# One layer of a streaming-encoder trunk on one core: gate and up weights, from the second strip on, split into a ring of four buffers, each strip at its own byte position

## The chip, the cores and the metric

The kernel runs on one core of a Trainium2 chip. The metric is the device time of one execution in microseconds (us). The core has five engines that run beside each other and wait for each other by semaphores: TensorE (PE; matrix products, with PEld for the loading of the stationary operand), VectorE (DVE), ScalarE (ACT), GpSimd (POOL) and SyncE (SP), which here issues the transfers from HBM. Matrix operands lie in SBUF (128 partitions, each a row of bytes), results in PSUM banks of 512 float32 per partition.

## The reference

All data are float32, 512 tokens of width 1024. What is computed is

```python
h = x + mixer(rms_norm(x))              # forgetting attention, latent attention, gates, output projection
hn = rms_norm(h, norm_ffn_g)
h = h + (silu(hn @ w_ffn_gate) * (hn @ w_ffn_up)) @ w_ffn_down     # hidden width 2816
y = rms_norm(h, norm_final_g)
```

The change concerns the two products `hn @ w_ffn_gate` and `hn @ w_ffn_up` (1024 by 2816 each).

## The kernel before

Float32 accuracy is made from three products in the type float32r. `split` (L98) writes a rounded copy `hi` of an operand (ScalarE, L101) and the remainder `lo = source - hi` (VectorE, L102). `mm3` (L124) adds hi·hi, hi·lo and lo·hi into one PSUM bank: three matmuls, the first operand stationary, the second streamed through the array. So each matmul is preceded by a load of 128 stationary columns, which is 512 bytes per partition, and streams up to 512 columns.

The feed-forward part starts after the mixer. `hTh` and `hTl` hold the normalised activations transposed, eight feature tiles of 128 features by 512 tokens, reached by `ht(k)`. The hidden width of 2816 is worked off in eleven strips of 256 (`NHC // 2`, loop at L935). For each strip the gate product goes into two PSUM banks (`pg`, tag a), the up product into two others (`pu`, tag b); then ScalarE takes silu of `pg`, VectorE multiplies by `pu`, and the result is split into `act[s]` (L947 to L951). The weights are the stationary operand: `strip` (L928) runs over the eight feature tiles k, over the two halves e of the strip and over the three products, 48 matmuls for one matrix of one strip. Strip 0 works in two halves of 256 tokens, because its activations arrive late; the other ten strips stream all 512 tokens, so that 20 times 48 matmuls of 512 columns follow each other.

`strip_weights` (L924) brings a matrix of a strip in two pieces of four feature tiles: `weights` (L130) takes a raw buffer (tag `wr`, two buffers), issues the transfer of 512 KB on SyncE's queue (L133), and `split_weights` (L136) takes a buffer `whi` and a buffer `wlo` (tags `wh` and `wl`, three of each) and splits. Strip 0 puts one piece into two buffers of tag `pt`. Tag `pt` has four buffers of `PTW` = 1664 float32 (6656 bytes), which the mixer used for attention weights and which hold the four normalised row tiles `hn` (L912) when the feed-forward part starts. After strip 0 they lie unused.

In the program's layout of SBUF the tiles that matter here (`wh`, `wl`, `pt`, the activations and `act`) all begin at byte 192 of a stretch of 512 bytes, and the blocks of 128 stationary columns inside them are whole multiples of 512 bytes further on. So every weight load of the feed-forward part starts at the same position in 512 bytes. The one large group of matmuls whose streamed operand starts elsewhere is the narrow input projection (`pms`, bank names `pm`, 424 columns): its weights lie 1696 bytes apart, so that feature tiles 0 to 3 start at bytes 192, 352, 0 and 160 of 512, and tiles 4 to 7 again.

The order on each engine is made by a planner that simulates the program; the mixer's matmuls are kept in written order (`pin`), the feed-forward part is left to the planner. Matmuls of one bank stay in order. The down product (L956 on) takes its weights by `weights` again, now as the streamed operand.

Of the kernel before, what the change touches and what calls it, by code (L numbers as in the profile page):

```python
# [8 lines left out]
F32 = mybir.dt.float32  # L9
F32R = mybir.dt.float32r  # L10
# [6 lines left out]
P = 128  # L17
D = 1024
S = 512
NT = S // P  # L20
KC = D // P
# [18 lines left out]
PTW = 3 * PTS + S  # L40
# [26 lines left out]
def tile_hybrid_fox_mla_block(  # L67
# [6 lines left out]
    nc = tc.nc  # L74
# [6 lines left out]
    w_ffn_gate, w_ffn_up, w_ffn_down = w_ffn_gate[0], w_ffn_up[0], w_ffn_down[0]  # L81

    big = ctx.enter_context(tc.tile_pool(name="big", bufs=1))
    ps = ctx.enter_context(tc.tile_pool(name="ps", bufs=1, space=bass.MemoryType.PSUM))

    def u8(shape, dtype, name):
        return big.tile(shape, dtype, name=name, tag="u8", bufs=17)
# [4 lines left out]
    def tmp(shape, name, dtype=F32):  # L92
        return big.tile(shape, dtype, name=name, tag="p", bufs=4)

    def bank(tag, name):
        return ps.tile([P, 512], F32, name=name, tag=tag, bufs=3 if tag == "a" else 5)

    def split(hi, lo, src, scale=None):  # L98

        if scale is None:  # L100
            one = nc.scalar.copy(out=hi, in_=src)  # L101
            two = nc.vector.tensor_tensor(out=lo, in0=src, in1=hi.bitcast(F32), op=ALU.subtract)  # L102
        else:
            one = nc.scalar.activation(out=hi, in_=src, func=AF.Copy, scale=scale)
            two = nc.vector.scalar_tensor_tensor(out=lo, in0=src, scalar=scale, in1=hi.bitcast(F32),
                                                 op0=ALU.mult, op1=ALU.subtract)
        if pin[1]:
            tc.keep_in_program_order(one)
            tc.keep_in_program_order(two)
# [4 lines left out]
    def matmul(*args, **kw):  # L114
        ins = nc.tensor.matmul(*args, **kw)  # L115
        if pin[0]:
            tc.keep_in_program_order(ins)
# [6 lines left out]
    def mm3(o, a, b, start, stop):  # L124

        matmul(o, lhsT=a[0], rhs=b[0], start=start, stop=False)
        matmul(o, lhsT=a[0], rhs=b[1], start=False, stop=False)
        matmul(o, lhsT=a[1], rhs=b[0], start=False, stop=stop)

    def weights(src, a, b, spare=False):  # L130

        raw = big.tile([P, a, b], F32, name="wraw", tag="wr", bufs=2)
        nc.sync.dma_start(out=raw, in_=src)  # L133
        return split_weights(raw, spare)
# [189 lines left out]
    for st in "f0 k0 f1 t0 k1 f2 t1 f3 t2 m1 t3 f4 t4 m2 t5 f5 f6 t6 f7 m3 t7 w0 w1".split():  # L324
        n = int(st[1])
# [10 lines left out]
        else:  # L336

            src = xf[n // 4][:, n % 4, :]
# [547 lines left out]
    def ht(k, cols=slice(None)):  # L886
        return hTh[k // 4][:, k % 4, cols], hTl[k // 4][:, k % 4, cols]
# [3 lines left out]
    for half in range(2):  # L891
        nn = slice(half * 512, (half + 1) * 512)
        wo = []
        for c in range(2):
            hi = u8([P, 4, 512], F32R, f"woh{half}{c}")
            lo = u8([P, 4, 512], F32R, f"wol{half}{c}")
            for d in range(2):
                raw = big.tile([P, 2, 512], F32, name="wraw", tag="wr", bufs=2)
# [4 lines left out]
        for t in range(NT):  # L903
            po = bank("a", "po")
            cols = slice(t * P, (t + 1) * P)
            for k in range(KC):
                c, kk = k // 4, k % 4
# [16 lines left out]
    def strip_weights(src, s, spare=False):  # L924
        return [weights(src[c * 512:(c + 1) * 512, s * 256:(s + 1) * 256].rearrange("(k p) n -> p k n", p=P), 4, 256,
                        spare and c == 1) for c in range(2)]

    def strip(po, w, cols):  # L928
        for k in range(KC):
            for e in range(2):  # L930
                c = slice(e * P, (e + 1) * P)
                mm3(po[e][:, cols], (w[k // 4][0][:, k % 4, c], w[k // 4][1][:, k % 4, c]), ht(k, cols),
                    k == 0, k == KC - 1)

    for s in range(NHC // 2):  # L935

        pg, pu = [bank("a", "pg") for _ in range(2)], [bank("b", "pu") for _ in range(2)]
        wg = strip_weights(w_ffn_gate, s)
        if s == 0:
            wu = strip_weights(w_ffn_up, s, spare=True)  # L940
            for cols in (slice(0, S // 2), slice(S // 2, S)):
                strip(pg, wg, cols)
                strip(pu, wu, cols)
        else:
            strip(pg, wg, slice(0, S))
            strip(pu, strip_weights(w_ffn_up, s), slice(0, S))
        for e in range(2):  # L947
            sg = tmp([P, S], "sg")
            last = nc.scalar.activation(out=sg, in_=pg[e], func=AF.Silu)
            nc.vector.tensor_tensor(out=sg, in0=pu[e], in1=sg, op=ALU.mult)  # L950
            split(act[s][:, e, 0, :], act[s][:, e, 1, :], sg)  # L951
# [4 lines left out]
    for half in range(2):  # L956
# [5 lines left out]
        po = [bank("b" if half == 0 or t == NT - 1 else "a", "pd") for t, _, _ in parts]  # L962
# [63 lines left out]
def build(inputs):  # L1026
    import numpy as _np
    import concourse.bacc as _bacc
    import concourse.tile as _tile
    from concourse import mybir as _mybir  # L1030

    nc = _bacc.Bacc("TRN2", target_bir_lowering=False, num_devices=1)
    inputs = dict(inputs)
    inputs["xT"] = inputs["x"][0].T
    inputs["norm_mix_gT"] = inputs["norm_mix_g"].reshape(KC, P).T
    arrays, args = {}, []
    for name, a in [(n, inputs[n]) for n in _INS] + list(_constants().items()):
        a = _np.ascontiguousarray(a)
        arrays[f"in_{name}_dram"] = a
        args.append(nc.dram_tensor(f"in_{name}_dram", a.shape, _mybir.dt.from_np(a.dtype), kind="ExternalInput").ap())  # L1040
    args.append(nc.dram_tensor("out_0_dram", _OUT[0], F32, kind="ExternalOutput").ap())
    with _tile.TileContext(nc, schedule_with_timeline_sim=True) as tc:
        tile_hybrid_fox_mla_block(tc, *args)
    return nc, arrays
# [8 lines left out]
```

## Time and profile before

| | |
|---|---|
| time, median of 3 runs | 749.67 us (748.59 to 749.82) |
| profiled execution | 749.56 us, span from first to last instruction 747.8 us |
| PE busy | 730.3 us, 98% of the span |
| DVE, ACT, POOL busy | 57%, 45%, 10% |
| gate and up products of strips 1 to 10 | 402.49 to 620.12 us of the span |
| down product | from 620.12 us, 120.90 us |

The times of the profile come from the profiled execution. A busy PE is not a measure of its pace, since matmuls are pipelined and a shown matmul lasts longer than the distance to the next one; the pace is read from starts, or from the chain of work that ended last, which gives the time from one piece to the next.

### The profile page before, as it was taken

How to read it: one execution, taken by the hardware profiler on the slowest of the kernel's cores; microseconds unless marked ns; L12 is line 12 of the kernel's file. 1: busy time of each engine (PE TensorE's matmuls, PEld its weight loads, DVE VectorE, ACT ScalarE, POOL GpSimd, SP SyncE). 2: the span in 40 equal slices, each digit the busy share in tenths (PEclk: the TensorE clock that was granted, in tenths of full speed). 3: DMA queues.
4: the chain of work that ended last, by engine and by line, in shares of the span. 5: the costliest groups of instructions: out<-in, count | busy, mean ns of one | idle time of the engine just before them, and what ended most of it. 6: DMA issues, size and time to landing. Idle time of an engine off the chain costs nothing.

```text
span 747.8 us, 9512 instructions
## 1 busy us (share of the span) xinstructions
PE 730.3 (98%) x3601; PEld 608.4 (81%) x3601; DVE 423.0 (57%) x818; ACT 335.9 (45%) x635; POOL 72.0 (10%) x88
## 2 busy tenths in 40 slices
PE   5999999999999999999999999999999999999996
PEld 3988777878888888887899888888888888888885
DVE  6998988666898986576644332333333233225214
ACT  7457977555675774534514232323232232213113
POOL 4242331012121020300000000000000000000000
PEclk9899999999999999999999999999999999999999
DMA  8512112131223222274302323333332323323212
GB/s 280 170 45 69 41 49 57 29 86 30 87 58 78 65 57 85 86 244 148 114 29 86 112 85 108 90 93 104 87 111 85 112 86 96 102 85 112 85 57 112
DMA packets 68941, 69.45 MB, mean 93 GB/s; under 512 B 3808, under 2 KB 58352, under 8 KB 68896
## 3 DMA queue, kind: packets, MB, share of 16 engines
q1 hardware_dynamic: 66240, 64.91, 29.3%
q10 hardware_dynamic: 1824, 3.38, 1.4%
q0 software_dynamic: 832, 0.57, 0.3%
q8 instruction: 28, 0.46, 0.2%
q14 instruction: 17, 0.14, 0.1%
HBM read 66.59 MB, written 2.10 MB: 92 GB/s over the span
## 4 chain that ended last, share of the span: by engine, by line
PE 90%; DVE 4%; ACT 2%; DMA 2%; issue 1%; SPq 0%
PE pg L115 26%; PE pd L115 16%; PE pu L115 16%; PE pqa L115 6%; PE pb L115 6%; PE sp L115 4%; PE po L115 4%; PE pva L115 3%; PE py L115 3%; PE pt L120 2%; PE pm L115 2%; DMA wraw<-in_w_out_dram 1%; DMA wraw<-in_w_in_dram 1%; PE pqb L115 1%; ACT sq L340 1%
## 5 line engine op out<-in xcount | busy, mean ns | idle before, releaser
L102 DVE TENSOR_TENSOR wlo<-wraw,whi 128x1024 fp32r<-128x1024 f32 x102 | 125.4, 1230 | 200.6 <-ACT whi L101 200.1
L101 ACT CAST whi<-wraw 128x1024 fp32r<-128x1024 f32 x102 | 106.8, 1048 | 214.4 <-PE pu L115 78.5
L115 PE MATMUL pd<-whi,act 128*128 128x512 f32 (+1 forms) x396 | 110.9, 366 | 0.0
L115 PEld LDWEIGHTS pd<-whi,act 128*128 128x128 f32 x396 | 71.6, 189 | 12.4
L115 PE MATMUL pd<-wlo,act 128*128 128x512 f32 (+1 forms) x198 | 72.5, 366 | 0.0
L115 PE MATMUL pg<-hTh,wlo 128*128 128x512 f32 (+1 forms) x192 | 71.4, 372 | 0.0
L115 PE MATMUL pu<-hTl,whi 128*128 128x512 f32 (+1 forms) x192 | 71.3, 371 | 0.0
L115 PE MATMUL pu<-hTh,whi 128*128 128x512 f32 (+1 forms) x192 | 71.3, 371 | 0.0
L115 PE MATMUL pu<-hTh,wlo 128*128 128x512 f32 (+1 forms) x192 | 71.3, 371 | 0.0
L115 PE MATMUL pg<-hTl,whi 128*128 128x512 f32 (+1 forms) x192 | 71.3, 371 | 0.0
L115 PE MATMUL pg<-hTh,whi 128*128 128x512 f32 (+1 forms) x192 | 71.1, 371 | 0.0
L115 PE MATMUL pg<-xTh,whi 128*128 128x512 f32 x128 | 52.4, 410 | 0.0
L115 PE MATMUL pg<-xTh,wlo 128*128 128x512 f32 x128 | 50.2, 392 | 0.0
L115 PE MATMUL pg<-xTl,whi 128*128 128x512 f32 x128 | 50.1, 391 | 0.0
L115 PEld LDWEIGHTS pd<-wlo,act 128*128 128x128 f32 x198 | 37.4, 189 | 6.1
L115 PEld LDWEIGHTS pu<-hTh,wlo 128*128 128x128 f32 x192 | 36.2, 188 | 6.3
L115 PEld LDWEIGHTS pg<-hTh,wlo 128*128 128x128 f32 x192 | 36.2, 188 | 6.3
L115 PEld LDWEIGHTS pu<-hTl,whi 128*128 128x128 f32 x192 | 36.2, 188 | 6.3
L115 PEld LDWEIGHTS pg<-hTl,whi 128*128 128x128 f32 x192 | 36.2, 188 | 6.2
L115 PEld LDWEIGHTS pg<-hTh,whi 128*128 128x128 f32 x192 | 36.2, 188 | 6.2
L115 PEld LDWEIGHTS pu<-hTh,whi 128*128 128x128 f32 x192 | 36.2, 188 | 6.1
L435 POOL TENSOR_SCALAR gate<-gate 128x512 f32<-128x512 f32 x16 | 28.2, 1762 | 116.8 <-ACT gate L433 116.5
(281 smaller groups left out, 1433.7 us busy)
## 6 DMA issues: line engine op xcount, KB each, us to landing
wraw<-in_w_in_dram SPq DMA_DIRECT2D x28, 512.0 KB, 3.9
wraw<-in_w_ffn_gate_dram SPq DMA_DIRECT2D x22, 512.0 KB, 3.7
wraw<-in_w_ffn_up_dram SPq DMA_DIRECT2D x22, 512.0 KB, 3.7
wraw<-in_w_ffn_down_dram SPq DMA_DIRECT2D x22, 512.0 KB, 3.7
wraw<-in_w_out_dram SPq DMA_DIRECT2D x8, 512.0 KB, 4.0
xf<-in_xT_dram SPq DMA_DIRECT2D x8, 256.0 KB, 5.1
wraw<-in_w_branch_b_dram SPq DMA_DIRECT2D x4, 512.0 KB, 3.5
wraw<-in_w_branch_a_dram SPq DMA_DIRECT2D x4, 512.0 KB, 3.3
```

Of the source, the lines that this page charges most:

```text
L101: one = nc.scalar.copy(out=hi, in_=src)
L102: two = nc.vector.tensor_tensor(out=lo, in0=src, in1=hi.bitcast(F32), op=ALU.subtract)
L115: ins = nc.tensor.matmul(*args, **kw)
L120: ins = nc.tensor.transpose(*args)
L340: tc.keep_in_program_order(nc.scalar.activation(out=dst, in_=src, func=AF.Square))
L435: nc.gpsimd.tensor_scalar(out=g, in0=g, scalar1=1e30, scalar2=None, op0=ALU.min)
```

## The change

From strip 1 on, each matrix of a strip is brought in three pieces of three, three and two feature tiles (transfers of 384, 384 and 256 KB) through the same raw buffers. Each piece is split into one buffer of tag `pt` that holds both `hi` and `lo`, 768 float32 (3072 bytes) apart; the four buffers of the tag are used in turn. Within its buffer a piece begins `place` float32 from the start. `places` has one entry for each of the 20 matrices, gate and up of strips 1 to 10 in turn: in bytes 0, 16, 32, 48, 64, 80, 96, 112, 128, 160, 192, 224, 256, 320, 384, 448, 8, 24, 40 and 0. The buffers' length is a multiple of 512 bytes, and so is the distance from hi to lo, so that all weight loads of one matrix start at the same position in 512 bytes, and each matrix has its own. The products, their number and their order are the same. Strip 0 keeps its code.

```diff
@@ -932,18 +932,35 @@
+    places = [0, 4, 8, 12, 16, 20, 24, 28, 32, 40, 48, 56, 64, 80, 96, 112, 2, 6, 10, 0]
+
+    def ring_strip(po, src, s, place):
+
+        for k0 in range(0, KC, 3):
+            n = min(3, KC - k0)
+            raw = big.tile([P, n, 256], F32, name="wraw", tag="wr", bufs=2)
+            nc.sync.dma_start(out=raw, in_=src[k0 * P:(k0 + n) * P, s * 256:(s + 1) * 256].rearrange("(k p) n -> p k n", p=P))
+            both = big.tile([P, PTW], F32R, name="wboth", tag="pt", bufs=4)
+            hi, lo = [both[:, place + 768 * i:place + 768 * i + n * 256].rearrange("p (k n) -> p k n", k=n) for i in range(2)]
+            split(hi, lo, raw)
+            for k in range(n):
+                for e in range(2):
+                    c = slice(e * P, (e + 1) * P)
+                    mm3(po[e], (hi[:, k, c], lo[:, k, c]), ht(k0 + k), k0 + k == 0, k0 + k == KC - 1)
+
     for s in range(NHC // 2):
 
         pg, pu = [bank("a", "pg") for _ in range(2)], [bank("b", "pu") for _ in range(2)]
-        wg = strip_weights(w_ffn_gate, s)
         if s == 0:
+            wg = strip_weights(w_ffn_gate, s)
             wu = strip_weights(w_ffn_up, s, spare=True)
             for cols in (slice(0, S // 2), slice(S // 2, S)):
                 strip(pg, wg, cols)
                 strip(pu, wu, cols)
         else:
-            strip(pg, wg, slice(0, S))
-            strip(pu, strip_weights(w_ffn_up, s), slice(0, S))
+            ring_strip(pg, w_ffn_gate, s, places[2 * s - 2])
+            ring_strip(pu, w_ffn_up, s, places[2 * s - 1])
```

## Rows read from the trace of the kernel before

**Rows 1.** The page: busy us of each engine, share of the span, instructions.

```profile
PE 730.3 (98%) x3601; PEld 608.4 (81%) x3601; DVE 423.0 (57%) x818; ACT 335.9 (45%) x635; POOL 72.0 (10%) x88
```

**Rows 2.** The page: chain of work that ended last, shares of the span.

```profile
PE 90%; DVE 4%; ACT 2%; DMA 2%; issue 1%; SPq 0%
```

**Rows 3.** The chain in order of time: start us, us, what, matmuls merged.

```profile
191.16 1.39 PE pqa L115 x6
...
383.87 0.87 PE ptr L120 x8
...
390.97 5.76 PE pg L115 x48
...
402.49 10.91 PE pg L115 x48
413.40 10.88 PE pu L115 x48
...
609.24 10.88 PE pu L115 x48
620.12 120.90 PE pd L115 x594
```

**Rows 4.** Windows: stretch, its us, busy us of each engine, PE clock, DMA share, GB/s.

```profile
20.20:23.00 2.80, 2.80 (x9) 2.61 (x9) 2.80 (x7) 0.20 (x1) 1.79 (x4) 0.50 1.01 310
24.70:26.00 1.30, 1.30 (x8) 1.26 (x7) 1.30 (x2) 1.30 (x4) 0.82 (x1) 1.00 0.08 25
402.49:620.12 217.63, 217.63 (x962) 180.25 (x961) 73.93 (x80) 61.65 (x80) 0.00 (x0) 1.00 0.33 97
```

**Rows 5.** Timeline inside strip 1: start us, duration, engine, instruction.

```profile
413.24 0.39 PE L115 MATMUL pu<-hTh,whi 128*128 128x512 f32 x1
413.24 0.19 PEld L115 LDWEIGHTS pu<-hTl,whi 128*128 128x128 f32 x1
...
413.46 0.39 PE L115 MATMUL pu<-hTl,whi 128*128 128x512 f32 x1
413.47 0.19 PEld L115 LDWEIGHTS pu<-hTh,wlo 128*128 128x128 f32 x1
```

**Rows 6.** Timeline of PE, narrow input projection, 424 columns, one matmul each row.

```profile
20.22 0.56 PE L115 MATMUL pm<-mlo,xTh 128*128 128x424 f32 x1
...
23.05 0.56 PE L115 MATMUL pm<-mhi,xTh 128*128 128x424 f32 x1
...
24.46 0.36 PE L115 MATMUL pm<-mlo,xTh 128*128 128x424 f32 x1
...
26.01 0.35 PE L115 MATMUL pm<-mhi,xTh 128*128 128x424 f32 x1
...
28.29 0.36 PE L115 MATMUL pm<-mhi,xTh 128*128 128x424 f32 x1
...
28.87 0.35 PE L115 MATMUL pm<-mhi,xTh 128*128 128x424 f32 x1
...
30.39 0.35 PE L115 MATMUL pm<-mhi,xTl 128*128 128x424 f32 x1
```

**Rows 7.** Groups of instructions, 402 to 620 us: busy us, mean ns, idle before, releasers.

```profile
L102 DVE TENSOR_TENSOR wlo<-wraw,whi 128x1024 fp32r<-128x1024 f32 x40 | 49.1, 1227 | 118.5 <-ACT whi L101 118.5
L101 ACT CAST whi<-wraw 128x1024 fp32r<-128x1024 f32 x40 | 41.9, 1048 | 116.6 <-PE pu L115 78.5 <-issue 34.4 <-PE pg L115 3.7
...
L102 DVE TENSOR_TENSOR act<-sg,act 128x512 fp32r<-128x512 f32 x20 | 12.9, 684 | 0.1
...
L101 ACT CAST act<-sg 128x512 fp32r<-128x512 f32 x20 | 11.5, 617 | 2.0 <-DVE sg L950 2.0
```

**Rows 8.** DMA issues: tile, queue, count, KB each, us from issue to landing.

```profile
wraw<-in_w_ffn_gate_dram SPq DMA_DIRECT2D x22, 512.0 KB, 3.7
```

**Rows 9.** Timeline of ACT at the turn of strips 1 and 2.

```profile
407.81 1.05 ACT L101 CAST whi<-wraw 128x1024 fp32r<-128x1024 f32 x1 [3.70 <-PE pg L115]
412.76 0.60 ACT L949 ACTIVATE sg<-pg 128x512 f32<-128x512 f32 x1 [3.89 <-PE pg L115]
```

## The prediction

> **What bounds the kernel now.** I read the page's busy times first, then the chain of work that ended last, then that chain in order of time, and only then the timeline. TensorE is busy 730.3 of 747.8 us, twice as long as ScalarE [rows 1], and 90% of the chain is its work [rows 2]. In order of time the chain shows the stretch of the change: one row of 48 matmuls follows the next, each 10.88 us long and each starting where the one before ends, from 402.49 to 620.12 us, when the down product starts at once [rows 3]. (The first has 10.91.) The window over that stretch says the same: PE busy for all of its 217.63 us, at the full clock, while VectorE works 73.93 us and ScalarE 61.65 [rows 4]. So nothing that feeds TensorE is late there, and the stretch can move in two ways only: the pace of a matmul changes, or something becomes late that is now early.
>
> The pace is 10.88 / 48 = 226.67 ns. At the clock of the window, its upper level of 2.4 GHz, 512 columns alone take 213.33 ns; 13.33 ns (32 cycles) are left over for each matmul. The halves of strip 0 have 256 columns and take 5.76 / 48 = 120.0 ns [rows 3], against 106.67: again 13.33. So this is a price for each matmul and not for each column. The timeline shows what is paired with each matmul: the load of the next stationary block starts within 10 ns of it and lasts 0.19 of the 0.23 us to the next one [rows 5].
>
> **Is it a price of address?** That is the question of this change, and the feed-forward part can't answer it, since all its loads start at the same byte of 512. The narrow input projection says something, because there the streamed operand starts elsewhere. At half clock (0.50, 1.2 GHz [rows 4]) eight matmuls of 424 columns take 23.05 - 20.22 = 2.83 us [rows 6], 353.8 ns each, where 424 columns alone take 353.3: the load costs nothing. At the full clock (424 columns: 176.67 ns) three positions follow [rows 6]:
> - byte 160: 24.46 to 26.01, eight in 1.55 us, 193.75 ns, a price of 17.1
> - byte 192, as everywhere: 26.01 to 28.29, twelve in 2.28 us, 190.0 ns, a price of 13.3
> - byte 352: 28.87 to 30.39, eight in 1.52 us, 190.0 ns, a price of 13.3
>
> So three lengths and two positions give 13.33 exactly, and one position gives 3.75 ns more. That one comes straight after the change of clock, and the row of byte 352 also begins dearer (28.29 to 28.87: three in 0.58 us, 193.3 each) before it settles. In the mixer, too, six matmuls in a disturbed stretch take 1.39 us, 231.7 each, all at byte 192 [rows 3]. I therefore read the 13.33 as the load's fixed share, and the extra 3 to 5 ns as what a sequence pays for some matmuls after something has changed. The other reading is the first rival.
>
> The Trainium skill bears on this: its page "SBUF — State Buffer", section "Who interferes with whom", gives TensorE two independent read ports, one for the streamed operand and one for the weight load, and says it never waits on anyone. By that no start address could matter and the sum of the pace is zero; but by that the load should be free at the full clock as well, and these rows show 13.33 ns. The rule is not the whole account, so the rivals on the address keep their chances.
>
> **The change, part by part**, against the profiled execution (749.56 us, 1.76 us more than its span; 0.11 below the median).
>
> *Places.* 18 of the 20 matrices start their loads at another byte than now: 18 x 48 = 864 matmuls; two keep it. The bounds of the unknown price per matmul: downward, the whole 13.33 goes, 864 x 13.33 = 11.5 us; upward, the disturbed pace of 231.7 lasts, 864 x 5.0 = 4.3 us. I take zero for settled pace, since byte 352 against 192 shows no difference, and one settling time for each matrix, because each changes the position: six matmuls at 5.0 ns, 0.03 us, at most 20 x 0.03 = 0.6 us; half of it, 0.3, is what I count.
>
> *Splits.* Six pieces for a strip in place of four. A cast of 1024 float32 takes 1048 ns, one of 512 takes 617; a subtraction 1227 and 684 [rows 7]. By halves between them 768 take 0.83 and 0.96 us. One matrix costs ScalarE 2 x 0.83 + 0.62 = 2.28 us (now 2.10) and VectorE 2 x 0.96 + 0.68 = 2.60 (now 2.45), in 10.88 us of TensorE. With 20 matrices this is 3.7 and 2.8 us more on engines that are idle two thirds of the stretch [rows 4]: nothing on the path. Without that cover a piece would cost 0.83 + 0.96 = 1.8 us.
>
> *Waits of the ring.* A piece may be cast when TensorE has finished the piece four before. Three pieces lie between, always 3 + 3 + 2 tiles in some order, which is one matrix: 10.88 us. Cast and subtraction need 1.8, so 9.1 us are to spare. Now there are three buffers of four tiles, two pieces or again 10.88 us between, and 1.05 + 1.23 needed: 8.6 to spare. The new wait is no tighter. Behind a waiting cast on ScalarE stands the silu and behind a waiting silu the next cast: silu waits for the end of the gate product as long as 3.89 us [rows 9], but the cast after it is due more than 8 us later. TensorE waits twice a piece, 20 more pieces, 40 more waits; the middle of each 10.88-us row now holds such a wait and each row is the same to 0.03 us [rows 3], so I count nothing, at most 0.03 us for each of 20: 0.6.
>
> *Transfers.* 60 on SyncE's queue in place of 40, the same bytes. 512 KB land 3.7 us after issue [rows 8]; 384 KB will need no more. A raw buffer is free when the piece two before is split, so the next transfer is issued 1.8 us after the end of piece c - 6, lands at 5.5 us, and its cast waits for the end of piece c - 4, 6.8 us or more after that of c - 6. It is early by 1.3 us, and a late one eats first into the 9.1. The DMA engines are a third busy [rows 4].
>
> *The ends.* In strip 1 the third piece and the next take the two buffers in which strip 0 keeps up weights, free only at 402.49; the third is needed two pieces later, at 402.49 + 8.16 = 410.65, and what ScalarE and VectorE have before it there are the two halves of the activation, 2 x (0.60 + 0.62) us on ScalarE [rows 7, 9] and about as much on VectorE. The first two pieces use buffers of the normalised rows, free since the last transposes end at 384.74 [rows 3]. At 620 the down product's first weights use the `wh` and `wl` buffers, which nobody has used since strip 0; there is nothing to gain, as TensorE already starts it at once.
>
> Sum: 749.56 + 0.3 = 749.9 us.
>
> **Rivals.**
>
> *A shifted load is dearer (slower).* If the 17.1 of byte 160 is the position's own, then a distance of 32 bytes between the starts of the two operands costs 3.75 ns on each matmul. For it: eight matmuls without settling [rows 6]. Against: the change of clock just before, and byte 352. At all 18 matrices: 864 x 3.75 = 3.2 us, 752.8. At the 11 matrices alone whose place is no multiple of 64 bytes: 528 x 3.75 = 2.0 us, 751.5. It decides from 1.7 ns on, averaged over the 864 (1.5 us). I give its middle, 752.
>
> *A shifted load is cheaper (faster).* The price exists only at the full clock, so the two streams compete for something; if that is a part of memory chosen by the low bits of the address, another position may avoid it. For it: zero at half clock. Against: it is the same for 256, 424 and 512 columns and for byte 352. If half of the 864 lose the whole price: 5.8 us, 744; if a third loses half: 1.9 us, 747.9.
>
> *The ring is late (slower).* If the planner puts casts behind silus so that one piece in each matrix comes late by a split (20 x 1.8) it would be 786; one such wait in strip 1 alone gives 752. With 9.1 us to spare I hold only the second for possible.
>
> *The positions aren't what the list says.* If the ring's buffers started elsewhere in 512 bytes, all 20 matrices would be shifted and the same prices would stand on 960 matmuls: 749.9 without a dependence, 753.2 if shifted loads are dearer. Both groups of buffers begin at byte 192 in the layout before, which speaks against it.
>
> **How the numbers follow.** A change of less than 0.2% (1.5 us) can't be told from none in this kernel. No dependence on place, with up to 0.6 us each for settling and waits: 0.47, between 749.2 and 751.1, nearly all of it the same. Dearer: 0.31, of which a tenth stays below 1.5 us. Cheaper: 0.17, of which a little stays above. Late ring: 0.05. That makes faster 0.17, same 0.47, slower 0.36. The range leaves out the farther part of the cheaper case and what lies beyond 754: from 745.0 to 753.8, the upward bound of 4.3 us included.
>
> **What would show it.** In the chain, each of the 20 rows of 48 matmuls again 10.88 us, plus at most 0.03 at its first matmuls: then place costs nothing. Rows that differ from each other by place and come back to 10.88 in the last one (byte 0 again) would prove the dependence; 11.06 at 32 bytes would be the dearer case, 10.24 a load without price. Idle time of PE at a piece's first matmul, with VectorE's remainder as its releaser, would be the late ring. The prediction is wrong if the 20 rows' sum leaves 217.6 by more than 1.5 us, or if anything before 402 or after 620 moves as much.

## The result: 0.57% slower, and every lost microsecond stands in the shifted rows

The changed kernel takes 753.13 us (median of 4 runs, 752.96 to 754.57) beside 749.13 us for the kernel before (748.59 to 749.82). The ratio is 1.0057 with a 95% interval of 1.004 to 1.0075.

The chain of work that ended last, in order of time, of the changed kernel (start us, us, what). The 20 matrices come in the order of `places`: 0, 16, 32, 48, 64, 80, 96, 112, 128, 160, 192, 224, 256, 320, 384, 448, 8, 24, 40 and 0 bytes.

```profile
401.23 10.91 PE pg L115 x48
412.13 10.89 PE pu L115 x48
423.02 11.19 PE pg L115 x48
434.21 11.20 PE pu L115 x48
445.41 11.19 PE pg L115 x48
456.60 11.12 PE pu L115 x48
467.73 11.24 PE pg L115 x48
478.97 11.20 PE pu L115 x48
490.16 11.20 PE pg L115 x48
501.36 11.20 PE pu L115 x48
512.57 11.00 PE pg L115 x48
523.57 11.19 PE pu L115 x48
534.76 10.88 PE pg L115 x48
545.64 11.20 PE pu L115 x48
556.84 11.16 PE pg L115 x48
568.00 11.00 PE pu L115 x48
579.00 11.07 PE pg L115 x48
590.07 11.10 PE pu L115 x48
601.16 11.20 PE pg L115 x48
612.36 10.88 PE pu L115 x48
623.25 120.90 PE pd L115 x594
```

Where all rows had been 10.88 [rows 3], only bytes 0, 16 and 256 have that now, to 0.03 us. Most others are at 11.20, which is 233.33 ns a matmul: 20.0 ns over the 213.33 of 512 columns, where it had been 13.33. A few rows lie between, from 11.00 to 11.16. The last row is at byte 0 and back at 10.88, so nothing drifts. The window over the stretch (columns as in [rows 4]) has no idle time of PE:

```profile
401.23:623.25 222.02, 222.02 (x961) 180.35 (x961) 79.93 (x102) 68.24 (x101) 0.00 (x0) 1.00 0.34 100
```

It is 4.39 us longer than before (217.63). The down product has its 120.90 us again. In this execution strip 1 began 1.26 us earlier than in the profile before, and what comes after the down product took 0.27 us more, which with rounding makes the span 3.4 us longer; the medians differ by 4.0.

The new splits (groups of instructions, 402 to 623 us, columns as in [rows 7]) cost what was expected of them and lie beside TensorE's work:

```profile
L102 DVE TENSOR_TENSOR wboth<-wraw,wboth 128x768 fp32r<-128x768 f32 x38 | 36.4, 959 | 71.6 <-ACT wboth L101 71.6
L101 ACT CAST wboth<-wraw 128x768 fp32r<-128x768 f32 x38 | 31.6, 833 | 69.1 <-PE pu L115 25.7 <-PE pg L115 21.1 <-DVE sg L967 19.4
```

### The profile page after: what moved, and what is told of

Its sections match the earlier page's. It is cut to its first block, busy times and chain, and to the rows that moved or that the text cites. A ratio compares the mean times of both kernels' runs of the same rounds, so it can differ in the third digit from the quotient of the medians.

```text
span 751.2 us, 9631 instructions
## 1 busy us (share of the span) xinstructions
PE 735.9 (98%) x3601; PEld 609.3 (81%) x3601; DVE 425.8 (57%) x838; ACT 340.3 (45%) x655; POOL 71.9 (10%) x88
## 4 chain that ended last, share of the span: by engine, by line
PE 87%; DVE 6%; DMA 3%; ACT 2%; issue 1%; SPq 0%; ACTq 0%; DVEq 0%
PE pg L115 25%; PE pu L115 16%; PE pd L115 16%; PE pqa L115 6%; PE pb L115 5%; PE sp L115 4%; PE po L115 4%; PE pva L115 3%; PE py L115 3%; PE pt L120 2%; DMA wraw<-in_w_out_dram 1%; DMA wraw<-in_w_in_dram 1%; PE pqb L115 1%; DMA wraw<-in_w_kv_up_dram 0%; PE ptr L120 0%
## 5 line engine op out<-in xcount | busy, mean ns | idle before, releaser
L102 DVE TENSOR_TENSOR wboth<-wraw,wboth 128x768 fp32r<-128x768 f32 (+1 forms) x60 | 52.1, 870 | 127.4 <-ACT wboth L101 127.4
L102 DVE TENSOR_TENSOR wlo<-wraw,whi 128x1024 fp32r<-128x1024 f32 x62 | 76.4, 1232 | 78.5 <-ACT whi L101 78.0
L101 ACT CAST wboth<-wraw 128x768 fp32r<-128x768 f32 (+1 forms) x60 | 45.7, 762 | 136.3 <-PE pu L115 60.6
L101 ACT CAST whi<-wraw 128x1024 fp32r<-128x1024 f32 x62 | 64.9, 1049 | 92.2 <-PE pd L115 63.0
L115 PE MATMUL pg<-hTh,wboth 128*128 128x512 f32 x320 | 101.6, 393 | 0.0
L115 PE MATMUL pu<-hTh,wboth 128*128 128x512 f32 x320 | 101.5, 393 | 0.0
L115 PEld LDWEIGHTS pg<-hTh,wboth 128*128 128x128 f32 x320 | 60.1, 188 | 13.8
L115 PEld LDWEIGHTS pu<-hTh,wboth 128*128 128x128 f32 x320 | 60.1, 188 | 13.8
L115 PE MATMUL pu<-hTl,wboth 128*128 128x512 f32 x160 | 63.0, 394 | 0.0
L115 PE MATMUL pg<-hTl,wboth 128*128 128x512 f32 x160 | 63.0, 393 | 0.0
```

## The experiments

The theories at the start: A, the price of a weight load depends on the distance between its start and the start of the streamed operand; B, it depends on the load's own start; C, the ring itself costs the time. The streamed activations and the ring's buffers start at the same byte of 512, except where a run moves the activations, so a place in bytes is also the distance from the start of the streamed operand to that of the load, modulo 512. A row of 48 matmuls is called cheap at 10.88 to 10.93 us and dear near 11.20, and rhythm stands for the pattern in which the starts of the matmuls repeat. Each chain below is in order of time, with start us, us and what, of the kernel named.

### The ring without places

```diff
-    places = [0, 4, 8, 12, 16, ...]
+    places = [0] * 20
```

> The ring kept as it is, every matrix at byte 0. Theory A (the price of a weight load depends on the distance between its start and the start of the streamed operand) and theory B (it depends on the load's own start alone) both give 20 rows of 48 matmuls at 10.88 us (10.91 for the first, which follows strip 0) and the time of the kernel before, 749.1 us, within 1 us. Theory C (pieces of three tiles, six transfers or the common buffer of hi and lo cost the time) gives rows that stay above 10.88 and a time near 753.

Measured: 749.19 us beside 749.04, ratio 1.0004 (0.9994 to 1.0014).

```profile
401.08 10.91 PE pg L115 x48
...
607.82 10.88 PE pu L115 x48
618.70 120.90 PE pd L115 x594
```

All rows are those of the kernel before. The ring, its smaller pieces and its 20 further transfers cost nothing that can be measured: C falls.

### The ring at one shifted place

```diff
+    places = [8] * 20
```

> The ring with every matrix at byte 32. In the changed kernel byte 32 took 11.19 us a matrix. A and B: every row 11.19, the stretch of 20 matrices 223.8 us where it was 217.6, the time 749.1 + 6.2 = 755.3 us. C: no more than with byte 0. If the price were one of changing the position from matrix to matrix, it would vanish here after the first few matmuls: 10.88 a row.

Measured: 755.45 us beside 749.04, ratio 1.0087 (1.007 to 1.0104).

```profile
401.75 11.19 PE pg L115 x48
...
614.54 11.20 PE pu L115 x48
```

The price does not fade. A matrix that stays at byte 32 pays 0.32 us each time, 6.67 ns a matmul, so it isn't a price of changing the place.

### The other places

```diff
+    places = [36, 44, 52, 60, 68, 72, 76, 84, 88, 92, 100, 104, 108, 116, 120, 124, 1, 3, 4, 0]
```

> The ring with the positions that the changed kernel left out, in bytes 144, 176, 208, 240, 272, 288, 304, 336, 352, 368, 400, 416, 432, 464, 480, 496, 16, 48, 64, 0 of 512 from the buffer's start. If the price repeats every 256 bytes, as 0 and 256, 64 and 320, 192 and 448 did, byte 272 takes 10.88 (as 16), 288 and 304 take 11.2 (as 32 and 48), 336, 352 and 368 take 11.1 to 11.2 (as 80, 96, 112), 416 takes 11.2 (as 160) and 480 takes 11.19 (as 224). If 512 is the period, these agree only by chance. Any row below 10.88 would be a position better than that of the kernel before; I expect none.

Measured: 754.87 us in one run. The last four places are bytes 4, 12, 16 and 0; the expectation had taken them for 16, 48, 64 and 0. In the order of the list: 10.89, 11.04, 11.13, 10.98, 11.20, 11.19, 11.20, 11.13, 11.24, 11.20, 11.20, 11.19, 11.04, 11.20, 11.20, 10.91, 11.15, 11.20, 11.20, 10.91. Five rows of it, bytes 144, 176, 272, 4 and 16:

```profile
402.79 10.89 PE pg L115 x48
413.68 11.04 PE pu L115 x48
...
446.82 11.20 PE pg L115 x48
...
580.72 11.15 PE pg L115 x48
...
603.07 11.20 PE pg L115 x48
```

The period of 256 holds for 288, 304, 336, 352, 368, 416, 432 and 480. It fails for 272, 400, 464 and 496 (16, 144, 208 and 240 have other prices), and byte 16 took 11.20 here, after byte 12, where the changed kernel had 10.89 after byte 0: one place has two prices. No place is below 10.88.

### The streamed operand shifted

```diff
-    c1 = big.tile([P, C_INVF], F32, name="c1", tag="c1", bufs=1)
+    c1 = big.tile([P, C_INVF + 8], F32, name="c1", tag="c1", bufs=1)[:, 0:C_INVF]
...
+    places = [0, 4, 8, 12, 16, 20, 24, 28, 32, 40, 48, 56, 64, 68, 72, 76, 2, 6, 10, 8]
```

> The activations and everything laid behind them begin 32 bytes later (byte 224 of 512), the ring's buffers stay at 192; positions in bytes 0, 16, 32, 48, 64, 80, 96, 112, 128, 160, 192, 224, 256, 272, 288, 304, 8, 40, 24, 32. Theory A: the cheap rows (10.88) move by 32 to bytes 32, 48, 288, 304 and the last 32; byte 224 takes 11.00 (as 192 did), byte 40 takes 11.07 (as 8), and 0 and 256 take about 11.19. Theory B: 0, 16, 256 and 272 stay at 10.88 and 32, 48 at 11.2. The down product, both of whose operands move, stays at 120.9 us in A.

Measured: 753.07 us in one run. Rows of bytes 0, 32, 48, 224 and 40:

```profile
402.03 11.20 PE pg L115 x48
...
424.19 10.90 PE pg L115 x48
435.10 10.89 PE pu L115 x48
...
524.29 11.00 PE pu L115 x48
...
601.43 11.07 PE pg L115 x48
```

The cheap rows moved with the activations: 0 is dear now, 32 and 48 are cheap, 288 and 304 too (10.88 and 10.89), 224 has the 11.00 of 192. A holds but for byte 272, 10.88 at a distance of 240, which had cost 10.98, and byte 16, 10.96 at 496, which had cost 10.91. The places at odd multiples of 8 say the same: byte 40, now at distance 8, took the 11.07 that byte 8 had taken, as A expects, and not its own 11.20; byte 24, now 8 bytes below the stream, took 11.20 where it had taken 11.10. Byte 8 took 11.09; its distance of 488 was not tried elsewhere. So the distance is what moves the price, and B falls.

### The kernel before with its weights shifted

```diff
-    shift = small([P, 112], "shift", bufs=1)
+    shift = small([P, 120], "shift", bufs=1)[:, 0:112]
```

> The kernel before, without the ring, with one change: the six split-weight buffers (tags wh and wl) begin 32 bytes later, at byte 224 of 512. If distance alone makes the price: the 20 matrices of strips 1 to 10 take 11.20 us each, the stretch 224.0 where it was 217.6 (+6.4); the down product, whose streamed weights now begin 32 bytes after the stationary activations, goes from 120.9 to about 124 (462 matmuls of 512 columns by up to 6.7 ns), and the mixer's gates and projections, about 770 matmuls of 512 columns already unsettled by 2 to 4 ns, add 2 to 4 us. Together 758 to 763 us. If the ring were needed for the loss (hi and lo in one buffer 3072 bytes apart, pieces of three tiles), the rows stay at 10.88 and the time at 749.

Measured: 758.18 us beside 748.72, ratio 1.013 (1.0107 to 1.0153). Windows over strips 1 to 10 and over the down product, columns as in [rows 4]:

```profile
402.32:626.31 223.99, 223.99 (x961) 180.36 (x961) 74.07 (x80) 61.76 (x80) 0.00 (x0) 1.00 0.33 94
626.31:749.55 123.24, 123.20 (x595) 101.87 (x593) 39.42 (x58) 31.27 (x48) 0.00 (x0) 1.00 0.26 86
```

One pad of 32 bytes in a kernel without the ring costs more than the whole change, 9.5 us: 6.4 in the strips, 2.3 in the down product, where the streamed operand was the one that moved, and under 1 us elsewhere. The 2 to 4 us expected of the mixer did not come. The down product stayed a little below the expected 124: from start to start its 462 matmuls of 512 columns went from 227.7 to 233.2 ns, 5.6 and not 6.7 more, and its 132 of 256 columns from 119.0 to 117.0.

### Only the remainder shifted

```diff
-            hi, lo = [both[:, place + 768 * i:place + 768 * i + n * 256] ... for i in range(2)]
+            hi, lo = [both[:, place + 776 * i:place + 776 * i + n * 256] ... for i in range(2)]
```

All places are 0.

> The ring with hi at byte 0 and lo 32 bytes further from the cheap position (3104 instead of 3072 bytes behind hi). If each load pays for itself, one load in three is dear: 10.88 + 16 x 6.67 ns = 10.99 us a matrix. If what counts is the rhythm of the whole sequence, one shifted load in three is enough to keep it from settling and the rows lie between 11.0 and 11.2, with a pattern of several matmuls. If the lo loads were hidden, 10.88.

Measured: 754.35 us in one run.

```profile
613.46 11.20 PE pu L115 x48
```

All rows but the first (11.18) are at 11.20: one shifted load in three costs as much as three. So a load doesn't pay by itself: what has a price is the sequence. The starts of the matmuls repeat 233, 239 and 228 ns here, and 227, 226, 227 at distance 0.

### Which place came before

```diff
+    places = [8, 4, 8, 4, 0, 4, 0, 4, 8, 0, 8, 0, 124, 4, 124, 4, 64, 68, 64, 60]
```

> The ring with positions in bytes 32, 16, 32, 16, 0, 16, 0, 16, 32, 0, 32, 0, 496, 16, 496, 16, 256, 272, 256, 240. Byte 16 took 10.88 us when byte 0 came before it and 11.15 when byte 496 did. If the matmuls before decide (the rhythm is kept when the step is small): 16 after 0 takes 10.88, 16 after 32 and after 496 takes about 11.15; 272 after 256 10.88; 0 always 10.88 to 10.91, whatever came before. If the place in the order (buffer, tile, matrix) decided, 16 would not follow its predecessor.

Measured: 751.98 us in one run. Byte 16 after 32, byte 0, byte 16 after 0, and byte 16 after 496:

```profile
413.96 11.20 PE pu L115 x48
...
447.56 10.88 PE pg L115 x48
458.44 10.88 PE pu L115 x48
...
546.13 10.88 PE pu L115 x48
```

Byte 16 is dear after 32 and cheap after 0; 272 after 256, and 240 and 496, which had cost 10.98 and 10.91, are cheap here too. My expectation of 11.15 for 16 after 496 was wrong, because it came from a row that was byte 4. Over all runs, nine rows of 512 columns have a distance of 16: six came after a cheap row and took 10.88 or 10.89, three after a dear one (32 twice, 12 once) and took 11.20. So at this distance a row keeps the pace of the row before. At others it doesn't: byte 0 is cheap after dear rows and byte 32 dear after cheap ones (11.19 here). Why a distance belongs to one kind or the other is open.

### Half of the columns loaded

```diff
+    places = [0] * 10 + [8] * 10
...
+                    full = k0 + k in (0, KC - 1)
+                    c = slice(e * P, e * P + (P if full else 64))
+                    mm3(po[e] if full else po[e][0:64, :], ...)
```

> The ring, ten matrices at byte 0 and then ten at byte 32. In the middle six of the eight feature tiles only the first 64 of 128 stationary columns are loaded (36 of 48 matmuls; half of these tiles' output is left out), while 512 columns are streamed as before. If the 13.33 ns and the 6.67 ns are both paid per loaded column, these 36 go to 213.33 + 6.67 = 220.0 ns at byte 0 and 223.3 at byte 32: 10.64 and 10.84 us a matrix (with 12 full ones at 226.67 and 233.3). If 13.33 is a fixed price of a matmul and only the extra is the load's: 10.88 and about 11.08. If both are fixed: 10.88 and 11.20.

Measured: 753.22 us in one run. Rows at byte 0 and at byte 32:

```profile
490.13 11.00 PE pg L115 x48
...
601.26 11.14 PE pg L115 x48
```

None of the three expectations holds. At byte 0 half a load is dearer than a whole one (11.00 against 10.88), at byte 32 a little cheaper (11.14 against 11.20). The price is not counted in loaded columns alone. The half loads also write only 64 of the 128 partitions of a bank, and no run separates the two.

### Half of the columns streamed

```diff
+        for cols in (slice(0, S // 2), slice(S // 2, S)):
+            for k0, n, hi, lo in pieces:
...
+                        mm3(po[e][:, cols], (hi[:, k, c], lo[:, k, c]), ht(k0 + k, cols), ...)
```

> The ring with each matrix worked in two halves of 256 tokens (96 matmuls of 256 columns in place of 48 of 512), positions in bytes 0, 16, 32 and so on in steps of 16 to 288, then 0. At distance 0 strip 0 ran at 120.0 ns: 11.52 us a matrix, and 11.36 with its weights 32 bytes on (117 to 118 ns, seen in the down product and strip 0 of the kernel with shifted buffers). If the price of a distance is a property of the two addresses alone, 32 and 48 should be dearer here too (120.0 + 6.7 = 126.7 ns, 12.2 us). If it is a rhythm between load and stream that also depends on the stream's length, the order of positions is another one here, with rows below 11.52 at 32. A piece that comes late would show as idle time of TensorE at a matrix's second piece.

Measured: 758.78 us in one run; only its rows matter, since 96 short matmuls replace 48. Bytes 0, 32 and 64:

```profile
401.76 11.52 PE pg L115 x96
...
424.64 11.36 PE pg L115 x96
...
447.31 10.88 PE pg L115 x96
```

With 256 columns distance 0 is among the dearest (120.0 ns) and 64 the cheapest: 10.88 / 96 = 113.33 ns, 6.67 over the columns' own 106.67. So the order of the places depends on the length of the stream; a price of two addresses alone is refuted.

### Each place entered from distance 0

```diff
+    places = [0, 36, 0, 44, 0, 48, 0, 52, 0, 56, 0, 60, 0, 2, 0, 1, 0, 32, 0, 100]
```

> The ring with every second matrix at byte 0 and between them the positions 144, 176, 192, 208, 224, 240, 8, 4, 128 and 400, so that each is entered from the cheap rhythm. If a position's price is its own: 144 takes 10.89, 176 11.04, 192 11.00, 208 11.13, 224 11.19, 240 10.98, 8 11.07, 128 and 400 11.20, as in the runs before. If the rhythm before decides: 240 takes 10.88 (as after 256), and others may fall too. Byte 0 returns to 10.88 to 10.91 each time in both. Byte 4: between 10.88 and 11.07.

Measured: 750.41 us in one run. Bytes 224, 240 and 4:

```profile
499.92 11.19 PE pu L115 x48
...
521.99 10.88 PE pu L115 x48
...
565.75 11.15 PE pu L115 x48
```

Both readings hold for a part of the places. 144, 176, 192, 208, 224 and 8 cost what they had cost (10.88, 11.04, 10.99, 11.13, 11.19, 11.07), 128 nearly (11.16 for 11.20); 240 and 400 fell to 10.88 from 10.98 and 11.20. Byte 4 costs 11.15, the same as after byte 496. Byte 0 came back to 10.88 to 10.93 every time.

### A kernel that uses it

```diff
-        hi = big.tile([P, a, b], F32R, name="whi", tag="pt" if spare else "wh", bufs=4 if spare else 3)
-        lo = big.tile([P, a, b], F32R, name="wlo", tag="pt" if spare else "wl", bufs=4 if spare else 3)
+            both = big.tile([P, 2112], F32R, name="wboth", tag="wh", bufs=3)
+            two = [both[:, place + 1024 * i:place + 1024 * (i + 1)] for i in range(2)]
...
+                     place=48) for c in range(2)]
...
+                        spare and c == 1, place=16 if s == 0 else 0) for c in range(2)]
```

> The kernel before, not the changed one: hi and lo of the split weights share three buffers whose length is a multiple of 256 bytes, and where 256 columns are streamed the distance between stationary and streamed operand is 64 bytes (modulo 256): strip 0 with its weights 64 bytes on, the mixer's value projection with its streamed weights 192 bytes on. Everything with 512 columns stays at distance 0. From the run with halves (113.3 ns at 64 against 120.0 at 0): the three full rows of strip 0 go from 5.76 to 5.44 us, the value projection's 192 matmuls gain up to 6.7 ns each, together up to 2.6 us: 746.5 to 748 us, at best 0.3% faster than before. If the rhythm does not settle in the value projection, which is cut by the attention's matmuls, only strip 0's 1.3 us.

> The same kernel with both positions put back to 0: the layout of the buffers alone. 749.0 us as before, strip 0's rows 5.76. Where the two differ, the distance alone is the cause.

Measured: with the distances 749.23 us, ratio to before 1.0006 (0.9998 to 1.0015); with the layout alone 749.77 us, 1.0013 (1.0004 to 1.0022). Strip 0's second gate row, all of it at distance 64, then with the layout alone:

```profile
390.91 5.65 PE pg L115 x48
```

```profile
392.73 5.76 PE pg L115 x48
```

A miss. This row went from 5.76 to 5.65 us, which is 117.7 ns and not 113.3, though the distance was that of the cheap row with halves; 0.1 us a row is nothing in the whole. In the up rows around it half of the loads lie at 320, which was not tried with 256 columns, so they may keep it from settling; that is not shown. The value projection's matmuls went from 124.2 to 121.8 ns from start to start, where up to 6.7 ns had been hoped for. The two kernels' intervals overlap, and neither beats the kernel before. Within this study no version does.

## Why the prediction was right and wrong, by its steps

The sum was 749.9 us, and 753.13 was measured.

**The bound.** Right. TensorE was busy all through the stretch before and after, so its pace was what could move the time by much.

**The ring, its waits, splits, transfers and ends.** Right: the ring at byte 0 takes 749.19 us and its rows stand at 10.88, the first at 10.91 as before. The cast and the subtraction of 768 columns, taken halfway between two rows as 0.83 and 0.96 us, measured 833 and 959 ns.

**One settling time for each matrix.** Right in kind and near in size where there is a cheap rhythm to settle in: the rows of byte 0 that follow another place take 10.88 to 10.93, so up to 0.05 us, where 0.03 had been the most. At the dear places nothing settles.

**"I take zero for settled pace."** This failed, and the whole loss is here: 4.39 us over 864 matmuls is 5.08 ns each, where the sum had 0 and one settling of at most 0.03 us a matrix. That 5.08 lies so near the upward bound of 5.0 is luck: the bound was the pace of six disturbed matmuls of the mixer at byte 192, and 5.08 is a mean over rows that cost 0 to 7.5 ns more. The first rival, a dearer shifted load, is what happened; its place and kind were right, its price of 3.75 ns too small (6.67 at distance 32) and its choice of 11 matrices wrong, since 64, 128 and 320 bytes are as dear as 32. It had been given 0.31 against 0.47, and what put it second was above all one comparison: byte 352 cost nothing in the narrow projection [rows 6]. There the load lay 160 bytes below the stream, which is 352 of 512 above it, and with 512 columns exactly this distance was the dearest of all, 11.24. The row was true and did not carry over: it had 424 columns, and the runs with halves show that the order of the distances changes with the length of the stream. The three lengths that all gave 13.33 had looked like a constant of the load. They are one of the rhythms that a sequence can fall into: 113.33, 226.67 and 233.33 ns are 6.67, 13.33 and 20.0 ns over the columns. Not all rows sit on such a level (11.00 to 11.16 are between). For 424 columns no run tried the places by themselves, but the trace before has a row that the comparison passed over. In the first feature tile, at byte 192 as well and at a granted clock of 1.00, ten matmuls take 1.93 us, 193 ns each, and not 190.0:

```profile
9.51 0.35 PE L115 MATMUL pm<-mhi,xTl 128*128 128x424 f32 x1
...
11.44 0.35 PE L115 MATMUL pm<-mhi,xTh 128*128 128x424 f32 x1
```

So byte 192 had two paces in this projection, nearly as far apart as the 17.1 and 13.3 that the prediction weighed, and 13.33 was not a fixed share of the load.

**The rule of two ports.** The prediction weighed the Trainium skill's page "SBUF — State Buffer", section "Who interferes with whom", which calls TensorE's two read ports independent and says that PE never waits on anyone. A pad of 32 bytes, which moved the split weights and small tiles behind them, cost 9.5 us, and the cheap places moved when the activations moved. The measurement decides: at the full clock the pace depends on where the two operands start relative to each other.

**The cheaper rival.** No place with 512 columns fell below 10.88, and 32 places of 16 bytes' step were looked at. Its idea, that another position may avoid the price, came true in part and for 256 columns alone: 6.67 ns in place of 13.33 at distance 64.

**What would show it.** The signs were well chosen: rows that differ by place and return to 10.88 at the last byte 0 are what the trace shows, byte 32 is beyond the 11.06 of the rival, and 10.24, a load without price, appears nowhere.

What stays open is the mechanism. Distance, the length of the stream, the form of the load and the matmuls before each change the rhythm, and no run separates what the two reads meet at. At distance 16 a row keeps the pace of the row before, but that isn't the whole rule: distance 240 took 10.98 after a row of 11.13 and 10.88 after one of 11.19.

## What to carry to other kernels

Where a stretch is bound by matmuls that each load their weights, the start of a tile in SBUF is a parameter of its time: 32 bytes of padding in a small tile cost this kernel 1.3%. Read the pace of long rows of equal matmuls in the chain before and after any change of layout, and where the rows are cheap, keep the distance between stationary and streamed operand when tiles are added or resized. A row at another length of stream is no evidence for this one.

## What the runs showed of the hardware that was not expected

- One dear load in three makes the whole sequence dear: 11.20 us for 48 matmuls, as with all three.
- With loads of 64 columns in place of 128 the rows at distance 0 became slower, 11.00 against 10.88.
- At distance 16 rows of 48 matmuls take 10.88 or 10.89 us after a cheap row and 11.20 after a dear one.
- At distance 64 matmuls of 256 columns ran at 113.33 ns and at distance 0 at 120.0; in strip 0 of the kernel with the distances the same distance gave 117.7.
- At half clock a matmul of 424 columns had no price beside its columns [rows 4, 6]; all the rhythms above are of the full clock.
